# Query and key of two attention pairs by seven products in the first stage, and a new plan of slots for the heads

## The chip, the cores and the metric

The kernel runs on one core of a Trainium2 chip. The metric is the time of one execution on the device in microseconds; a kernel's time is the median of its runs. Of five engines four compute: PE (TensorE, matrix products and transposes), DVE (VectorE), ACT (ScalarE) and POOL (GpSimd); SP (SyncE) issues most of the transfers between DRAM and the on-chip memory. Each engine takes its own instructions in order, and waits with them for what others have to finish first.

## What is computed

One layer of a decoder on 512 tokens of width 2048, in float32. The reference, cut to what matters:

```python
h = rms_norm(x, g_mix)
z = h @ w_in                      # 2048 x 7168
aq, ak, av, rq, rk, rv, rg = split(z)
aq = rotate(rms_norm(heads(aq)) * q_norm)   # 8 heads of 128, attention
ak = rotate(rms_norm(heads(ak)) * k_norm)
a_out = moba_attention(aq, ak, av)          # causal softmax attention
rq, rk = rotate(heads(rq)), rotate(heads(rk)) * 128 ** -0.5
r = retention_chunkwise(rq, rk, rv)         # decayed q k^T v, 8 heads
r_out = silu(rg) * (rms_norm(r) * g_ret)
x = x + concat(a_out, r_out) @ w_o
x = x + (silu(rms_norm(x) @ w_gate) * (rms_norm(x) @ w_up)) @ w_down
x = x + (p @ w_ple_proj) * sigmoid(rms_norm(x) @ w_ple_gate + b)
```

## The kernel before

**Products in three parts.** A float32 number is split into a high and a low part (`split`, L51: the high part on ACT, L54, the low one on DVE, L55), and each product is three matmuls, high by high, low by high, high by low (`mm3`, L72, through L63). A matmul of 512 columns is the unit in which the work is counted below. Weights come from DRAM into `raw`, and their parts are `wh` and `wl`.

**Seven products.** A `Group` (L267) multiplies a matrix by 1024 columns of weights with seven products of half matrices in place of eight. Sums of weight quarters are formed by DVE (`raw<-raw`, L81), the factors of the left side are formed once, and each product goes to two PSUM banks named after X, Y or Z, which `evac` adds into the parts of the result. A group is 7 x 4 units of 12 matmuls, 336. The sums for some later weights (w_gu among them) are formed in DRAM, by moves that POOL issues (`summed`, `move`, L144 to L156).

**Stage 1** (`beside`, L603) computes h from x, the query and key of attention pair 0 in the plain way (`Plain`, L500, 8 units of 24 matmuls), and three groups: the values of the attention, those of the retention, and the gate (`kinds`, L598). Pair 0's query and key are stored to DRAM (`zd`), the values and gates too (`vd`, `sgd`, L596).

**The heads' stage.** Heads go in pairs: four pairs of attention (i = 0 to 3), four of retention (i = 4 to 7). For each pair but the first, `projection` (L684) makes query and key of both heads: 8 units of weights, of which `weights` (L671) keeps three ready, by four accumulators; each accumulator's six matmuls in a unit are one *slot*, so that a projection has 32 slots and 192 matmuls, and seven of them 224 slots. `tick` (L654) counts the slots. At each, the pieces that a plan of numbers has put there (`at_slot`, `heads`, L966) are written into the program ahead of the slot's matmuls. In this stage PE's order is the program's order. So the projection of one pair runs between the pieces of the pair before it, and a piece whose input is late stops PE.

For attention the pieces are (`attend`, L811): `turned`, twice, four 128x128 transposes of query or key into `tp` and a split into `qkH` and `qkL`; `scores` for each of four query blocks into `at`, with DVE's mask (L830), maximum (L832) and scale of it (L834), ACT's exponential into `pt` (L837) and DVE's reciprocal and scaling (L838, L839); `weights_turned`, the transposes of `pt` and their split into PH and PL; `result`, the product with v. Before them `qk_attn` (L768) rotates the pair's four token blocks: `z` (L781) and two `m` (L784) with the rope tables, the reduction of squares (L791), the sum of z and m (L81) and the norm's scale of the keys on ACT (L798). The tables (`rope`, L717 and L720) are made once, from `cs`, `sn` and `sides` that SP loads at the start of the stage (L703 to L715). In the retention `qk_ret` (L864) copies the accumulator, swaps the halves of each head by two transfers on ACT's queue (L876, L877), and rotates.

Each finished pair is turned into factors for the product with w_o (`mixed`, L960): sums and splits on DVE and ACT whose results go to DRAM (`spill`, L214) through four buffers `o`. Behind the heads stand p @ w_ple_proj (L1010 to L1027; its result `pp` is copied out of PSUM by ACT, L1023) and the first group of w_o, whose first 16 slots (`take_over`, L1033) still carry the last pieces.

## Time and profile before

| | us |
|---|---|
| runs | 2341.53, 2346.53, 2344.79 |
| median | 2344.79 |
| profiled execution, its own time | 2341.56 |
| span of the profile | 2339.80 |
| stage 1 with its three groups | 0 to 282 |
| heads' stage, attention pairs | 282 to 541 |
| heads' stage, retention pairs and p @ w_ple_proj | 541 to 714 |
| w_o, feed-forward and the last gate | 714 to 2339.8 |

The profile is of one execution. The busy time of an engine counts its instructions without waits; PEld is the loading of a weight into PE, which runs beside a matmul. The chain that ended last is followed backwards from the last instruction, at each step to what released it; its shares say on what the time lies. A row of the windows has the stretch, its length, then busy time and number of instructions for PE, PEld, DVE, ACT and POOL, the clock granted to PE (1.00 is full), the busy share of the DMA engines, and GB/s. A row of the waits has who waited for what: the sum, how often, and the longest. A row of the timeline has start, length, engine, line, operation, and the idle time before it with what ended it.

### The profile page before, as it was taken

How to read it: one execution, taken by the hardware profiler on the slowest of the kernel's cores; microseconds unless marked ns; L12 is line 12 of the kernel's file. 1: busy time of each engine (PE TensorE's matmuls, PEld its weight loads, DVE VectorE, ACT ScalarE, POOL GpSimd, SP SyncE). 2: the span in 40 equal slices, each digit the busy share in tenths (PEclk: the TensorE clock that was granted, in tenths of full speed). 3: DMA queues.
4: the chain of work that ended last, by engine and by line, in shares of the span. 5: the costliest groups of instructions: out<-in, count | busy, mean ns of one | idle time of the engine just before them, and what ended most of it. 6: DMA issues, size and time to landing. Idle time of an engine off the chain costs nothing.

```text
span 2339.8 us, 29408 instructions
## 1 busy us (share of the span) xinstructions
PE 2307.1 (99%) x10493; PEld 1899.2 (81%) x10493; DVE 1896.3 (81%) x2585; ACT 1200.1 (51%) x1792; POOL 105.3 (5%) x135
## 2 busy tenths in 40 slices
PE   9999999999999999999999999999999999999999
PEld 7888877778887888888888888888888878888877
DVE  8888586666667897888988888889879887788798
ACT  8644454444445566545554554455445443447643
POOL 0000011101011000000000000000000000000000
PEclk9999999999999999999999999999999999999999
DMA  6634736778766879477557754765596775869863
GB/s 241 237 129 169 224 117 175 201 204 255 203 195 235 309 270 366 147 225 237 164 153 229 241 147 157 239 220 155 185 395 201 253 300 198 300 228 360 291 206 126
DMA packets 184099, 519.72 MB, mean 222 GB/s; under 512 B 20496, under 2 KB 33424, under 8 KB 179856
## 3 DMA queue, kind: packets, MB, share of 16 engines
q1 hardware_dynamic: 167296, 463.30, 55.6%
q0 software_dynamic: 13952, 50.34, 10.1%
q10 hardware_dynamic: 2704, 4.20, 0.7%
q8 instruction: 82, 1.34, 0.2%
q14 instruction: 65, 0.53, 0.1%
HBM read 411.86 MB, written 147.85 MB: 239 GB/s over the span
## 4 chain that ended last, share of the span: by engine, by line
PE 81%; DVE 10%; DMA 5%; issue 2%; ACT 2%; SPq 0%; POOL 0%; ACTq 0%; DVEq 0%
PE Y L63 30%; PE Z L63 19%; PE X L63 18%; PE acc L63 9%; DVE wl L55 3%; PE at L63 2%; DVE raw L81 2%; PE tp L68 2%; ACT wh L54 1%; DMA raw<-in_w_dn 1%; DMA raw<-in_w_gu 1%; DMA mix<-o 1%; DMA a<-o 1%; DMA mr<-zr 0%; DVE t L78 0%
## 5 line engine op out<-in xcount | busy, mean ns | idle before, releaser
L54 ACT ACTIVATE wh<-raw 128x1024 fp32r<-128x1024 f32 (+1 forms) x728 | 769.9, 1059 | 853.4 <-PE Y L63 304.3
L55 DVE TENSOR_TENSOR wl<-raw,wh 128x1024 fp32r<-128x1024 f32 (+1 forms) x728 | 885.6, 1218 | 300.1 <-ACT wh L54 297.0
L63 PE MATMUL Y<-wh,s 128*128 128x512 f32 (+1 forms) x1656 | 522.8, 389 | 0.4 <-ACT wh L54 0.4
L81 DVE TENSOR_TENSOR raw<-raw 128x1024 f32<-128x1024 f32 x332 | 399.9, 1217 | 15.2 <-DMA raw<-in_w_dn 5.5
L63 PE MATMUL Z<-wh,s 128*128 128x512 f32 (+1 forms) x1164 | 367.4, 389 | 0.2 <-ACT wh L54 0.2
L63 PEld LDWEIGHTS Y<-wh,s 128*128 128x128 f32 x1656 | 310.1, 188 | 65.0 <-ACT wh L54 1.5
L63 PE MATMUL Y<-wl,s 128*128 128x512 f32 (+1 forms) x828 | 323.5, 391 | 1.7 <-DVE wl L55 1.7
L63 PE MATMUL X<-wh,s 128*128 128x512 f32 x1008 | 319.6, 390 | 2.9 <-ACT pp L1023 2.7
L63 PEld LDWEIGHTS Z<-wh,s 128*128 128x128 f32 x1164 | 218.0, 188 | 44.9 <-ACT wh L54 0.6
L63 PE MATMUL Z<-wl,s 128*128 128x512 f32 (+1 forms) x582 | 229.1, 394 | 2.1 <-DVE wl L55 2.1
L63 PEld LDWEIGHTS X<-wh,s 128*128 128x128 f32 x1008 | 189.5, 188 | 43.1 <-ACT pp L1023 3.4
L63 PE MATMUL X<-wl,s 128*128 128x512 f32 x504 | 197.3, 391 | 0.6 <-DVE wl L55 0.5
L63 PEld LDWEIGHTS Y<-wl,s 128*128 128x128 f32 x828 | 155.5, 188 | 35.0 <-DVE wl L55 3.3
L63 PE MATMUL Y<-wh,r 128*128 128x512 f32 x504 | 165.7, 390 | 1.3 <-ACT wh L54 1.1
L63 PE MATMUL acc<-h,wh 128*128 128x512 f32 x512 | 160.3, 394 | 0.8 <-DVE m L784 0.8
L63 PE MATMUL acc<-wh,h 128*128 128x512 f32 x384 | 130.1, 398 | 1.4 <-DVE m L784 1.1
L63 PEld LDWEIGHTS Z<-wl,s 128*128 128x128 f32 x582 | 109.3, 188 | 26.6 <-DVE wl L55 4.7
L63 PE MATMUL Z<-wh,r 128*128 128x512 f32 (+1 forms) x356 | 116.7, 388 | 0.0
L63 PEld LDWEIGHTS X<-wl,s 128*128 128x128 f32 x504 | 94.7, 188 | 21.0 <-DVE wl L55 1.6
L63 PEld LDWEIGHTS Y<-wh,r 128*128 128x128 f32 x504 | 94.4, 188 | 21.3 <-ACT wh L54 2.1
L63 PEld LDWEIGHTS acc<-h,wh 128*128 128x128 f32 x512 | 92.4, 188 | 17.7 <-ACT z L798 1.2
L63 PE MATMUL acc<-h,wl 128*128 128x512 f32 x256 | 100.3, 392 | 0.0
(225 smaller groups left out, 2887.1 us busy)
## 6 DMA issues: line engine op xcount, KB each, us to landing
raw<-in_w_gu SPq DMA_DIRECT2D x172, 512.0 KB, 5.7
raw<-in_w_dn SPq DMA_DIRECT2D x85, 512.0 KB, 6.1
a<-o SPq DMA_DIRECT2D x154, 256.0 KB, 4.9
raw<-in_wqk SPq DMA_DIRECT2D x63, 512.0 KB, 4.6
s<-a SPq DMA_DIRECT2D x21, 1536.0 KB, 7.5
raw<-in_w_vg SPq DMA_DIRECT2D x48, 512.0 KB, 4.9
raw<-in_w_ow SPq DMA_DIRECT2D x32, 512.0 KB, 5.5
xin<-x SPq DMA_DIRECT2D x60, 256.0 KB, 6.0
```

The lines of the kernel that those rows point to most:

```text
L54: return (nc.scalar.activation(H, src, AF.Copy), nc.vector.tensor_tensor(L, src, H.bitcast(F32), op=ALU.subtract))
L55: nc.vector.tensor_tensor(L, src, H.bitcast(F32), op=ALU.subtract))
L63: ins = nc.tensor.matmul(*args, **kw)
L68: ins = nc.tensor.transpose(o, a, ident)
L81: nc.vector.tensor_tensor(o, a, b, op=ALU.add)
```

## The change

The query and key of attention pairs 1 and 2 (of 0 to 3; the second and third) are computed in stage 1 by a fourth group of seven products (`pairs`), between the values of attention and those of retention. Their blocks are stored to DRAM (`zd[1]`, `zd[2]`), and their norms are computed there: eight stores, 32 squares with a sum on ACT. The heads' stage has five projections, of pair 3 and of the four of retention, 160 slots; the products for w_ple_proj are slots 161 to 176, and the first of w_o 177 to 192. Pairs 1 and 2 are loaded at slots 6 and 24 (four transfers each, behind the split of a unit of weights), and their blocks rotated in place from slots 12 and 27, by the same steps as before. Blocks of pair 0 go through the same function at the start of the stage, with its squares taken in stage 1. The plan now counts slots from the start of the stage. The high part of the retention's query and key is split later (`begin`); the swap of halves is done by two copies on ACT from PSUM. Seven products' parts 5, 3 and 2 of six mixed pairs are spilled through the four `rm` buffers. In the first w_o group the PSUM banks are asked for in the order X0, Z0, Z1, X1. PH and PL are two buffers zeroed once. Of 24 moves for w_gu 14 are issued in stage 1. Matmuls, transposes included, are 10493 before and 10445 after.

```diff
-    def spill(where, k, wait=1):
+    def spill(where, k, wait=1, other=None):
         def sink(p):
-            o = ev_tile("o", 4, (P, 2, 256), dt=F32R)
+            o = other((P, 2, 256)) if other and p in "532" else ev_tile("o", 4, (P, 2, 256), dt=F32R)
             store = lambda: nc.sync.dma_start(where[p][:, k].bitcast(F32), o.bitcast(F32))
             return o[:, 0, :], o[:, 1, :], lambda: later(wait, store) if wait else store()
...
             if first:
-                self.bank[k] = [pools.get("chain" + k, pools["chain"]).tile([P, T], F32, name=k + str(b), tag=k + str(b))
-                                for b in range(2)]
+                def bank(k, b):
+                    return pools.get("chain" + k, pools["chain"]).tile([P, T], F32, name=k + str(b), tag=k + str(b))
+                if self.spread and p == "1":
+                    x = bank("X", 0)
+                    self.bank["Z"] = [bank("Z", 0), bank("Z", 1)]
+                    self.bank["X"] = [x, bank("X", 1)]
+                elif not (self.spread and p == "5"):
+                    self.bank[k] = [bank(k, b) for b in range(2)]
...
+    def pairs():
+        def finish(th, nh, b, part, _):
+            tb = 2 * th + b
+            t = part
+            if (th, nh) == (0, 0):
+                t = ev_tile("o", 4, name="zq")
+                nc.scalar.activation(t, part, AF.Copy)
+            later(1, lambda: nc.sync.dma_start(zd[1 + nh][tb], t))
+            sq = ev_tile("o", 4, name="sq")
+            ms = stat.tile([P, 4], F32, name=f"ms{nh}_{tb}", bufs=1)
+            for j in range(4):
+                c = slice(j * HD, (j + 1) * HD)
+                nc.scalar.activation(sq[:, c], t[:, c], AF.Square, accum_out=ms[:, j:j + 1])
+            nc.vector.tensor_scalar(ms, ms, 1.0 / HD, eps1[:, tb:tb + 1], op0=ALU.mult, op1=ALU.add)
+            power(ms, ms, 4)
+            known[1 + nh][tb] = ms
+        return evacuate(finish)
...
-    kinds = [values(0), values(1), gates()]
-    groups = [Group(lambda kh, nh, u, j=j: w_vg[j, kh, nh, u], range(4), s_h, kinds[j]) for j in range(3)]
-    groups[0].next, groups[1].next = groups[1:]
+    kinds = [values(0), pairs(), values(1), gates()]
+    groups = [Group(lambda kh, nh, u, j=j: w_vg[j, kh, nh, u], range(4), s_h, kinds[j]) for j in range(4)]
+    for j in range(3):
+        groups[j].next = groups[j + 1]
     groups[0].pinned = True
...
+        if i >= 56 and i % 4 == 0 and i < 112:
+            move(gu_moves.pop(0), lead[0])
...
-        pieces.setdefault(slot[0] + n, []).append(fn)
+        assert n > slot[0]
+        pieces.setdefault(n, []).append(fn)
...
-    stream = [wqk[i, u] for i in range(1, 2 * NPAIR) for u in range(NC // 2)] + [pT] + [w_pp[n] for n in range(NS)]
+    tags = ["bd"] * 2 + ["c", "l1"] * (6 * NPAIR)
+
+    stream = [wqk[i, u] for i in range(1, NPAIR + 2) for u in range(NC // 2)] + [pT] + [w_pp[n] for n in range(NS)]
...
-            if gu_moves and slot[0] > 40:
+            if gu_moves and slot[0] > 18 and len(stream) % 2:
...
-    z0 = ap.tile([P, NB, 2, 256], F32R, name="z0", tag="v")
-    for b in range(NB):
-        nc.sync.dma_start(z0[:, b].rearrange("p c e -> p (c e)").bitcast(F32), zd[b])
+    def load_pair(i, by=None):
+        z = raw_pair()
+        for b in range(NB):
+            ins = nc.sync.dma_start(z[b // 2][:, b % 2], zd[i][b])
+            if by is not None:
+                paced(ins, by)
+        blocks[i] = [z[b // 2][:, b % 2] for b in range(NB)]
+        return ins
+
+    blocks = {}
...
+    def in_place(i, b, made, norms):
+        of = blocks[i][b]
+        sq = squares(of) if i == 0 else None
+        m = rm_tile("m", (P, 2, 2, 2, HD // 2))
+        z = of.rearrange("p (s h d) -> p s h d", s=2, h=2)
+        whole, *halves = turn(z, m, of, b)
+        for step in halves + [whole]:
+            step()
+        norms.append(norm(b, sq) if i == 0 else known[i][b])
+        made.append(rotated(z, m, norms[b]))
...
-            accs = [z0[:, b].rearrange("p c e -> p (c e)").bitcast(F32) for b in range(NB)]
+            for b in range(NB):
+                in_place(0, b, made, norms)
+        elif i < NPAIR - 1:
+            at_slot((6, 24)[i - 1], lambda: load_pair(i, lead[0]))
+            for b in range(NB):
+                at_slot((12, 27)[i - 1] + b, lambda b=b: in_place(i, b, made, norms))
...
-            nc.scalar.activation(z, acc, AF.Copy)
-            half = HD // 2
-            nc.scalar.dma_start(m[:half], z[half:])
-            nc.scalar.dma_start(m[half:], z[:half])
...
+            z, m = both[f // 2][:, f % 2], rm_tile("mr")
+            nc.scalar.activation(m[:half], acc[half:], AF.Copy)
+            nc.scalar.activation(m[half:], acc[:half], AF.Copy)
+            nc.vector.tensor_tensor(z, acc, cs, op=ALU.mult)
             nc.vector.tensor_tensor(m, m, sn, op=ALU.mult)
             nc.vector.tensor_tensor(z, z, m, op=ALU.add)
-            H, L = qk_pair()
-            split(H, L, z)
-            made.append((H, L))
-
-        for f, acc in enumerate(projection(False)):
-            evac(f, acc)
+            made.append(parted(z) if i == 2 * NPAIR - 1 else z)
...
+    ATTEND = (((1, four(4), four(8), 16), (10, four(14), four(18), 26)),
...
-        at_slot(17 if i < NPAIR else 20 if i == NPAIR else 8, lambda: v.append(v_of(i)))
...
-            plans = ((12, (15, 16, 19, 20), (19, 20, 23, 24), 27), (21, (25, 26, 39, 40), (29, 30, 42, 43), 46))
-            if i == 0:
-                plans = ((19, (22, 23, 26, 27), (26, 27, 30, 31), 33), (28, (34, 35, 39, 40), (39, 40, 43, 44), 47))
-            for j, (turns, steps_s, steps_w, last) in enumerate(plans):
+            for j, (turns, steps_s, steps_w, last) in enumerate(ATTEND[i]):
...
+        at_slot(MIXED[i], lambda: mixed(i, out))
...
-            if n:
+            if n == NS - 1:
+                t = ev_tile("o", 4, name="pp")
+            elif n:
...
+    groups[-1].ends = groups[0].spread = True
```

How the instructions stand now. On PE, where stage 1 ends and the heads' stage begins, before (Y is a bank of the last group, acc the projection's accumulators, h its left side):

```order
L63 MATMUL Y_2317<-wl,h 128x512
L63 MATMUL Y_2317<-wh,h 128x512 x2
L63 MATMUL Y_2317<-wl,h 128x512
L63 MATMUL Y_2317<-wh,h 128x512
L63 MATMUL acc<-wh,h 128x512
L63 MATMUL acc<-wl,h 128x512
L63 MATMUL acc<-wh,h 128x512 x2
L63 MATMUL acc<-wl,h 128x512
```

After (zr are the rotated blocks of pair 0, tp the PSUM tile for transposes):

```order
L63 MATMUL Y_2959<-wl,h 128x512
L63 MATMUL Y_2959<-wh,h 128x512 x2
L63 MATMUL Y_2959<-wl,h 128x512
L63 MATMUL Y_2959<-wh,h 128x512
L68 MATMUL tp<-ident,zr 128x128 x4
L63 MATMUL acc<-wh,h 128x512
L63 MATMUL acc<-wl,h 128x512
L63 MATMUL acc<-wh,h 128x512 x2
L63 MATMUL acc<-wl,h 128x512
L63 MATMUL acc<-wh,h 128x512
L68 MATMUL tp<-ident,zr 128x128 x4
```

The four transposes of pair 0's query have moved from behind 18 slots of projection to ahead of the first; those of the key stand one slot later.

On SP, the loads at the start of the heads' stage, after (sg is the gate's store of the last products, zr<-z_0_190 to z_3_193 the four loads of pair 1):

```order
L623 DMA sg<-e_2616 128x512
L623 DMA sg<-e_2617 128x512
L711 DMA raw<-in_wqk 128x1024
L753 DMA sides<-in_qk_norm 128x256
L757 DMA sides<-in_mask_c 128x128
L761 DMA cs<-in_rope_c 128x512
L762 DMA sn<-in_rope_c 128x512
L801 DMA v<-v_148 128x2x256 x4
L766 DMA zr<-z_0_190 128x512
L766 DMA zr<-z_1_191 128x512
```

The tables' loads stand behind the last two stores of gates, as before. The loads of pair 0, which stood behind them, are earlier now, and those of pair 1 have come in behind the values.

On DVE, in the first head of the stage, from the split of the first weights (PL) to the scaled weights of the third and fourth query block (pt, 128x384 and 128x512), before:

```order
L55 TENSOR_TENSOR PL<-tp,PH 128x128
L830 TENSOR_TENSOR at<-at,sides 128x128
L832 TENSOR_REDUCE mx<-at 128x1
L834 TENSOR_SCALAR mx<-mx,rs 128x1
L55 TENSOR_TENSOR PL<-tp,PH 128x2x128
L830 TENSOR_TENSOR at<-at,sides 128x128
L838 RECIPROCAL sm<-sm 128x1
L832 TENSOR_REDUCE mx<-at 128x1
L839 TENSOR_SCALAR pt<-pt,sm 128x384
L834 TENSOR_SCALAR mx<-mx,rs 128x1
L838 RECIPROCAL sm<-sm 128x1
L839 TENSOR_SCALAR pt<-pt,sm 128x512
```

After, from the mask of the third query block on; its pt comes seven rows behind the last of these (zr and m are blocks of pair 1 in rotation):

```order
L911 TENSOR_TENSOR at<-at,sides 128x128
L81 TENSOR_TENSOR zr<-zr,m 128x512
L832 TENSOR_TENSOR m<-zr,rope 128x4x64 x2
L830 TENSOR_TENSOR zr<-zr,rope 128x512
L81 TENSOR_TENSOR zr<-zr,m 128x512
L913 TENSOR_REDUCE mx<-at 128x1
L911 TENSOR_TENSOR at<-at,sides 128x128
L55 TENSOR_TENSOR wl<-raw,wh 128x1024
L55 TENSOR_TENSOR PL<-tp,PH 128x2x128
L830 TENSOR_TENSOR zr<-zr,rope 128x512
L81 TENSOR_TENSOR zr<-zr,m 128x512
L55 TENSOR_TENSOR qkL<-tp,qkH 128x512
```

Between mask and pt there now stands the rotation of pair 1, beside the splits of weights and of the second head's query and key. And in slots 28 to 32, after, up to the scaled weights of the third query block (zr is pair 2, z<-acc the projection of pair 3):

```order
L830 TENSOR_TENSOR zr<-zr,rope 128x512
L832 TENSOR_TENSOR m<-acc,rope 128x4x64 x2
L830 TENSOR_TENSOR z<-acc,rope 128x512
L832 TENSOR_TENSOR m<-acc,rope 128x4x64 x2
L915 TENSOR_SCALAR mx<-mx,ms_3_1957 128x1
L830 TENSOR_TENSOR z<-acc,rope 128x512
L830 TENSOR_TENSOR zr<-zr,rope 128x512
L919 RECIPROCAL sm<-sm 128x1
L81 TENSOR_TENSOR zr<-zr,m 128x512
L919 RECIPROCAL sm<-sm 128x1
L81 TENSOR_TENSOR zr<-zr,m 128x512
L920 TENSOR_SCALAR pt<-pt,sm 128x384
```

Two rotations, one from DRAM and one from accumulators, are interleaved ahead of that pt.

185 lines of the change are left out of this document (109 added, 76 removed), and 3 rows, old and new, of the table RETAIN.

## The prediction

> **What bounds the kernel now.** I read the page first: the span, the busy times, and the chain that ended last.
>
> ```profile
> span 2339.8 us, 29408 instructions
> PE 2307.1 (99%) x10493; PEld 1899.2 (81%) x10493; DVE 1896.3 (81%) x2585; ACT 1200.1 (51%) x1792; POOL 105.3 (5%) x135
> PE 81%; DVE 10%; DMA 5%; issue 2%; ACT 2%; SPq 0%; POOL 0%; ACTq 0%; DVEq 0%
> ```
>
> PE is busy 2307.1 of 2339.8 us, so the time is the number of matmuls times their pitch plus 32.7 us in which PE stands. A change pays only by fewer matmuls or fewer stalls. So the next views are the windows by stage and the waits of PE in the two parts of the heads' stage.
>
> ```profile
> 145.00:222.00 77.00, 76.46 (x336) 62.98 (x336) 62.73 (x63) 37.29 (x41) 0.00 (x0) 1.00 0.51 164
> ...
> 282.00:541.00 259.00, 248.29 (x1196) 202.42 (x1196) 179.32 (x416) 120.77 (x238) 40.68 (x41) 1.00 0.63 182
> 541.00:714.00 173.00, 169.09 (x835) 141.86 (x833) 116.05 (x217) 85.21 (x187) 18.21 (x25) 0.99 0.74 227
> ```
> ```profile
> PE tp L68 <- DVE pt L839: 5.1, 7, 1.5
> PE acc L63 <- DVE m L784: 1.9, 3, 0.8
> PE at L63 <- DVE PL L55: 1.5, 1, 1.5
> PE tp L68 <- ACT z L798: 0.8, 2, 0.4
> ```
> ```profile
> PE X L63 <- ACT pp L1023: 2.7, 2, 1.8
> PE acc L63 <- DVE wl L55: 2.3, 1, 2.3
> ```
>
> The first windows row is one group of seven products in stage 1: 336 matmuls, PE idle 0.54 of 77.00 us. In the attention part (second row) PE stands 10.7 us, mostly for the softmax steps of DVE; the first fence of waits is of that part, the second of 541 to 730. The waits named are short: 1.5 us at most there.
>
> **The matmuls.** Two projections of 192 matmuls leave the heads' stage, 384 together, and one group of 336 comes to stage 1: 48 fewer, all of 512 columns. The chain gives the pitch, and the price of opening a group.
>
> ```profile
> 84.92 10.88 PE Z L63 x48
> ...
> 140.81 3.41 DVE raw L81 x3
> 145.40 5.51 PE Z L63 x23
> ```
>
> 48 matmuls take 10.88 us (0.2267 each): −10.9. One more group opens with a short wait on the sums of weights: I take the 0.54 us of the windows row, +0.6. **Stage 1: −10.3.** The new group's sums (16 more on DVE) and 14 of the 24 moves of w_gu that now run there hide under PE, since DVE was busy 62.73 of 77.00 us and the DMA engines 0.51; if the cover fails, 0 to +2, kept for the range.
>
> **The start of the heads' stage** is where I see the largest cost. In the program's order PE now meets the four transposes of pair 0's q directly behind the last product of stage 1; before, 18 slots of projection (a slot is six matmuls) stood between. PE takes its instructions in order, so what the transposes wait for, everything waits for. They need all four rotated blocks, these need the rope tables, and the tables need cs, which SP issues behind the last two stores of gates; those need the last product itself. So this chain cannot start earlier than stage 1's end. Its length stands in the trace of before, where it was covered:
>
> ```profile
> 281.81 0.39 PE L63 MATMUL Y<-wh,h 128*128 128x512 f32 x1
> ```
> ```profile
> 283.93 0.94 SPq L596 DMA_DIRECT2D sg<-e  x2
> ...
> 286.46 0.38 SPq L711 DMA_DIRECT2D cs<-in_rope_c  x1
> ```
> ```profile
> 286.46 5.71 DMA cs<-in_rope_c
> ```
> ```profile
> 292.26 1.29 DVE L717 TENSOR_TENSOR rope<-cs,sides 128x512 f32<-128x512 f32 x2 [1.25 <-DMA cs<-in_rope_c]
> 293.47 1.22 DVE L55 TENSOR_TENSOR wl<-raw,wh 128x1024 fp32r<-128x1024 f32 x1
> 294.61 1.42 DVE L720 TENSOR_TENSOR rope<-sn,sides 128x256 f32<-128x256 f32 x4
> 295.95 0.68 DVE L781 TENSOR_TENSOR z<-z,rope 128x512 f32<-128x512 f32 x1
> 296.55 0.68 DVE L791 TENSOR_REDUCE ms<-sq 128x4 f32<-128x512 f32 x1
> ...
> 300.55 1.76 DVE L784 TENSOR_TENSOR m<-z,rope 128x256 f32<-128x256 f32 x5
> 302.23 0.67 DVE L791 TENSOR_REDUCE ms<-sq 128x4 f32<-128x512 f32 x1
> ...
> 304.82 1.28 DVE L81 TENSOR_TENSOR z<-z,m 128x512 f32<-128x512 f32 x2
> ```
>
> From starts to starts: cs issued 286.46, landed 292.17, first table 292.26. Two table products 293.47 − 292.26 = 1.21; four 295.95 − 294.61 = 1.34; then of the changed kernel's order eight m (1.68 / 5 = 0.336 each, 2.69), four z (0.60 each, 2.40) and four sums (0.60 each, 2.40, by z's pitch). Together 10.04: the blocks are ready at 302.3. The reductions and weight splits that lay between before are done earlier or later now, so I leave them out. PE's last product ends its turn at 281.81 + 0.23 = 282.04: an idle stretch of 20.3 us. What it replaces is the 0.8 us for z and 0.4 for e (a wait listed in the same view): **+19.1**, from 16 (an emptier DMA lands cs in less than its 5.71) to 22.
>
> After so long a rest I expect the clock at half. The trace shows what stalls do to it:
>
> ```profile
> 714.31 0.50 PE L63 MATMUL X<-wh,s 128*128 128x512 f32 x1 [0.96 <-ACT pp L1023]
> ...
> 717.76 0.50 PE L63 MATMUL X<-wh,s 128*128 128x512 f32 x1 [1.77 <-ACT pp L1023]
> ```
> ```profile
> 719.20:722.50 3.30, 3.30 (x10) 2.70 (x10) 2.37 (x7) 1.37 (x2) 1.76 (x2) 0.50 1.05 424
> ...
> 500.00:503.30 3.30, 3.30 (x18) 2.74 (x17) 2.96 (x9) 1.46 (x4) 0.52 (x1) 1.00 0.35 74
> ```
>
> Two waits of 0.96 and 1.77 us at the first group behind the heads were followed by 3.3 us at a granted clock of 0.50; half the work of such a stretch is lost, **+1.7** here, up to 3.4 if it holds for two. The Trainium skill, page "TensorE: Matmul & The Clock Gate", section "Part 1: The HAM clock gate", says that the clock halves after at least one idle window of about 3.4 us and recovers after as much busy time. By that rule the idle start costs the same 1.7, while waits of 0.96 and 1.77 would not have halved it: this trace disagrees there, and by the page alone the 1.7 gained at the first w_ow group (below) would not come, which makes the sum 1.7 worse. I go by the trace.
>
> **The first heads' softmax.** Pair 1's blocks come from DRAM at slot 6, are rotated in slots 12 to 15 of the plan, and in DVE's order this rotation stands among the first head's mask, maximum and scaling steps. DVE also takes them in order. Before, between the mask of the third query block and its scaled weights lay this:
>
> ```profile
> 321.33 0.29 DVE L830 TENSOR_TENSOR at<-at,sides 128x128 f32<-128x128 f32 x1
> 321.65 0.56 DVE L832 TENSOR_REDUCE mx<-at 128x1 f32<-128x384 f32 x1
> ...
> 324.20 0.41 DVE L839 TENSOR_SCALAR pt<-pt,sm 128x384 f32<-128x384 f32 x1
> ```
> ```profile
> 320.65 0.40 PE L63 MATMUL acc<-wh,h 128*128 128x512 f32 x1
> ...
> 327.99 0.49 PE L68 MATMUL tp<-ident,pt 128*128 128x128 f32 x3
> ```
> ```profile
> z<-z SPq DMA_DIRECT2D x8, 256.0 KB, 4.9
> ```
>
> That is 3.3 us of DVE, with 3.4 to spare before PE wanted them at 327.99. Now the same stretch of DVE holds two z and four sums (0.60 each), two m (0.336 each), a weight split (1.14), two qkL (0.60 each, as z), a PL split, two masks (0.29) and two maxima (0.56 and a little more) beside the small steps: 9.4 us by the pitches above, 6.1 more, 2.7 beyond the slack. Ahead of it the rotation stands on its load: this follows a split that is itself behind the first exponential, which I put at 311.7 on before's clock, plus 4.9 is about 317. The first weights' PL behind that comes at 319.9, and PE's slot 10 needs its transpose buffer at some 317: 2.9. The second, ten instructions later, holds slot 11 by 3.8. Together **+9**. Bounds: 0, if loads land early enough that DVE clears the rotation while PE is still in slots 4 to 8 (its share of that stretch is then below one); 12, if each is 1 us later.
>
> The same again in slots 28 to 32: between mask and weights lie pair 2's rotation, pair 3's accumulators (four z, eight m) and the first mixing, 14 us by the same pitches against 7.3 that PE's work covers before (320.65 to 327.99): some 7. With it go the three waits of PE for m, 1.9, at the ends of projections, of which only one projection remains: I take **+6**, from 0 to 10. Other heads keep four slots between scores and weights; I leave their waits as they are.
>
> **What goes elsewhere.** At the first w_ow group the banks are given so that X takes those copied earlier: the 2.7 us for pp goes, and the 1.7 of half clock behind it, **−4.4** (0 if the next wait on POOL's store or a weight takes its place). The retention's half swaps by two copies on ACT instead of a copy and two transfers.
>
> ```profile
> mr<-zr ACTq DMA_DIRECT2D x24, 128.0 KB, 5.1
> ...
> 684.78 0.69 DVE L879 TENSOR_TENSOR zr<-zr,ropeT 128x512 f32<-128x512 f32 x1 [2.19 <-DMA mr<-zr]
> ```
>
> A landing of 5.1 us leaves the chain; ACT, busy 85.21 of 173.00 us there, has room for 32 half copies. DVE's 2.19 is what made the split late for which PE waited 2.3: **−2.5** (0 to −4, if its half clock goes as well). Parts of the mixing kept in another buffer take some waits for stores away: **−1.5** (0 to −4).
>
> Sum: −10.3 + 19.1 + 1.7 + 9 + 6 − 4.4 − 2.5 − 1.5 = +17.1. On the profiled execution (2341.56) that is 2358.7; this stands 3.2 below the runs' median of 2344.79, on which it is 2361.9. I take **2360 us**. About 0.2% (4.7 us) is what a measurement of this kernel can tell from no change; runs of before spread by 5.0.
>
> **The rivals.** *The collisions don't occur (0.17).* DVE has 80 of 259 us free in the attention part and its order is only a queue; if loads land early, the 9 and 6 vanish, and m's 1.9 goes: about +2, 2346. For it: the waits of before are all short. Against: the rows of the order.
>
> *Faster (0.15).* The rotations leave the ends of the projections, where accumulators held PE, and run between, so that the attention's waits (5.1 + 1.9 + 1.5 = 8.5) go as a whole, without collisions: 2344.8 − 10.3 + 20.8 − 4.4 − 2.5 − 1.5 − 8.5 = 2338. It decides if pair 1's rotation is through DVE before slot 8's masks, and pair 2's before slot 28.
>
> *DVE becomes the bound (0.15).* Splits, rotations and softmax put more on DVE in slots 33 to 48 than PE needs for them (118% by my count of its instructions at these durations). With some 22 us of PE there, 18% is +4, and the queues behind lose as much again: with the start 2370.
>
> That fewer matmuls are run is certain from the counts (10493 to 10445); no rival is left there.
>
> **How the numbers follow.** My forecast has 0.53 and its own range is 2350 to 2366. The range of 8 in 10 reaches to most of the faster and slower rivals: 2339 to 2371. Faster 0.15 (the second rival), same 0.17 (the first), slower 0.68 (0.53 + 0.15).
>
> **What would show it.** At the end of stage 1, one idle stretch of PE of 16 to 22 us in front of a transpose, with DVE's sum named as releaser, then a row at clock 0.50. Waits of PE for PL and pt at slots 10 to 12, two to four us each, and in slots 28 to 32. No wait for pp at the first w_ow group. Stage 1 longer by one group (77.0 us), the heads' stage shorter by 87 of matmuls, less its stalls. I am wrong if that first stretch is below 10 us, or if the waits of the attention part stay below 1.5 us each.

## The result, and the profile after

| | before | after |
|---|---|---|
| median of 4 runs, us | 2343.16 | 2365.44 |
| lowest and highest | 2340.91, 2346.53 | 2362.40, 2365.76 |
| ratio, 95% interval | | 1.0088 [1.0076, 1.0099] |
| profiled execution, its own time | 2341.56 | 2362.40 |
| its span | 2339.8 | 2360.6 |
| start of the last product of stage 1 | 281.81 | 359.59 |
| start of the first product of w_o (X) | 714.31 | 732.66 |

The change made the kernel 22.3 us slower; the forecast was 2360 in a range of 2339 to 2371, with 0.68 on slower. Repeated (the last experiment) it was 1.0087 [1.0074, 1.0099], 18.9 us.

The starts in the table cut the program into three parts. Stage 1 is 77.78 us longer, the heads' stage 59.43 shorter (432.50 to 373.07), the rest 2.45 longer (1625.49 to 1627.94): +20.8, the difference of the two spans. The 384 matmuls that left the heads' stage are worth 384 x 0.2267 = 87.05, so without new stalls it would have come to 345.45; it is 27.6 above that. That is the loss to explain. The rest of the program, which the change hardly touches, was between 1624.3 and 1631.0 us in all the traces below, so small effects are read from the heads' stage and not from the sum.

The page after, its first lines:

```profile
span 2360.6 us, 29420 instructions
PE 2300.4 (97%) x10445; PEld 1896.0 (80%) x10445; DVE 1928.0 (82%) x2601; ACT 1230.6 (52%) x1882; POOL 116.2 (5%) x135
```

PE is 6.7 us less busy and the span 20.8 longer: PE stands 60.2 us where it stood 32.7. The windows after, of the new group (`pairs`, 128.6 to 205.5), of a stretch of two later groups and of the heads' stage:

```profile
128.60:205.50 76.90, 76.47 (x338) 63.05 (x336) 60.05 (x63) 41.36 (x84) 7.95 (x9) 1.00 0.49 158
...
222.00:299.00 77.00, 76.57 (x338) 62.89 (x337) 62.31 (x63) 37.70 (x41) 12.68 (x9) 1.00 0.69 219
...
359.80:732.60 372.80, 334.78 (x1645) 279.28 (x1645) 265.04 (x579) 194.14 (x413) 33.52 (x44) 0.95 0.61 186
```

The first two rows are as dense as the group's row of before, though squares run on ACT beside the one and moves for w_gu beside the other. The third row holds the loss: 38.0 us in which PE is not busy, and a granted clock of 0.95 in place of 1.00. The waits of PE after, from 359 to 745 (sum, times, longest):

```profile
PE tp L68 <- DVE zr L81: 17.9, 1, 17.9
PE tp L68 <- DVE pt L920: 11.6, 4, 8.3
PE tp L68 <- DVE r L1022: 4.7, 2, 3.8
PE tp L68 <- DVE PL L55: 3.3, 1, 3.3
```

Before, 18 waits of 1.5 us at most, but for one of 2.3, made 13.8 us in this stage. Now waits at four places make most of 38, and each stands where PE's order meets a transpose. The first is at the start; the timeline after, PE and SP and DVE merged:

```profile
361.71 0.94 SPq L623 DMA_DIRECT2D sg<-e  x2
...
364.21 0.38 SPq L761 DMA_DIRECT2D cs<-in_rope_c  x1
...
369.51 1.29 DVE L774 TENSOR_TENSOR rope<-cs,sides 128x512 f32<-128x512 f32 x2 [1.43 <-DMA cs<-in_rope_c]
...
372.06 2.76 DVE L832 TENSOR_TENSOR m<-zr,rope 128x256 f32<-128x256 f32 x8
...
377.16 2.49 DVE L81 TENSOR_TENSOR zr<-zr,m 128x512 f32<-128x512 f32 x4
377.89 2.28 PE L68 MATMUL tp<-ident,zr 128*128 128x128 f32 x4 [17.92 <-DVE zr L81]
379.83 0.77 PE L63 MATMUL acc<-wh,h 128*128 128x512 f32 x1
```

This is the chain of the prediction, step for step: stores of gates, cs issued behind them, tables, eight m, four z, four sums. From the last product (359.59) to the first of the projection it is 20.24 us, where it was 0.77. The four transposes start with the first sum and then take the blocks as the sums end, which is why the idle time shown is 17.9 and the loss more.

The second place is the first head's softmax. DVE after, from the rotation's start on its load to the scaled weights:

```profile
393.13 1.44 DVE L832 TENSOR_TENSOR m<-zr,rope 128x256 f32<-128x256 f32 x4 [0.80 <-DMA zr<-z]
...
396.84 0.29 DVE L911 TENSOR_TENSOR at<-at,sides 128x128 f32<-128x128 f32 x1
397.05 0.68 DVE L81 TENSOR_TENSOR zr<-zr,m 128x512 f32<-128x512 f32 x1
...
401.32 0.41 DVE L55 TENSOR_TENSOR PL<-tp,PH 128x256 fp32r<-128x256 f32 x1
...
405.68 0.42 DVE L920 TENSOR_SCALAR pt<-pt,sm 128x384 f32<-128x384 f32 x1
```
```profile
401.88 0.63 PE L68 MATMUL tp<-ident,zr 128*128 128x128 f32 x4 [3.25 <-DVE PL L55]
...
406.24 0.52 PE L68 MATMUL tp<-ident,pt 128*128 128x128 f32 x3 [2.34 <-DVE pt L920]
```

From the mask (396.84) to the end of the scaled weights DVE takes 9.3 us, with hardly a gap. Before it was 3.3. PE, in the second fence, stands first for PL and then for pt. The third place is slots 28 to 32, DVE and then PE:

```profile
449.49 0.68 DVE L830 TENSOR_TENSOR z<-acc,rope 128x512 f32<-128x512 f32 x1
450.09 0.68 DVE L830 TENSOR_TENSOR zr<-zr,rope 128x512 f32<-128x512 f32 x1
...
455.26 0.41 DVE L920 TENSOR_SCALAR pt<-pt,sm 128x384 f32<-128x384 f32 x1
```
```profile
455.81 0.87 PE L68 MATMUL tp<-ident,pt 128*128 128x128 f32 x3 [8.35 <-DVE pt L920]
```

The accumulators of pair 3 (z<-acc) and pair 2 (zr) alternate ahead of the pt for which PE waits 8.35 us. The fourth was not foreseen. Near the end of the heads' stage PE waits for r, the result of a retention head. POOL, DVE and PE there:

```profile
704.56 1.09 POOL L1116 DMA_DIRECT2D pp<-pp  x2 [0.44 <-ACT pp L1115]
705.67 1.06 POOL L84 TENSOR_TENSOR rs<-ms,neghalf 128x4 f32<-128x4 f32 x1
```
```profile
703.88 0.20 DVE L1018 TENSOR_SCALAR ms<-ms 128x4 f32<-128x4 f32 x1
...
708.34 0.87 DVE L1022 SCALAR_TENSOR_TENSOR r<-r,rs,sg 128x128 f32<-128x128 f32 x3
```
```profile
708.73 1.26 PE L68 MATMUL tp<-ident,r 128*128 128x128 f32 x4 [3.75 <-DVE r L1022]
```

The sum ms is ready at 704.08 (703.88 + 0.20). Its inverse root (L84) is POOL's, and stands behind stores of pp in POOL's queue until 705.67. That is 1.6 us; POOL's root takes 1.06, and DVE, which has the split of a weight and of a key to do first, comes to r another 1.6 later. The granted clock (third column from the end) behind the wait at 401.88, behind the one at 406.24, and behind the one for r:

```profile
401.90:407.10 5.20, 2.86 (x16) 2.19 (x17) 4.72 (x12) 3.77 (x10) 0.00 (x0) 1.00 0.35 102
407.50:410.50 3.00, 3.00 (x11) 2.41 (x10) 0.89 (x2) 1.55 (x2) 0.00 (x0) 0.50 0.00 0
...
708.00:713.90 5.90, 5.17 (x14) 4.06 (x15) 4.29 (x13) 2.97 (x8) 0.19 (x1) 0.50 1.03 418
```

The wait of 3.25 us at 401.88 left the clock at 1.00. Behind the start and the wait of 8.35 it is 0.50 too (377.9 to 382.5, 455.8 to 460.8). Counted from the rows of PE's matmuls against the pitch at full clock (0.2267 for 512 columns, 0.135 for a transpose), the four stretches lost, in the order of time, 1.6, 1.5, 2.5 and 2.7 us, 8.3 together.

### The profile page after: what moved, and what is told of

It is laid out like the page before. It is cut to its first block, busy times and chain, and to the rows that moved or that the text cites. A ratio compares the mean times of both kernels' runs of the same rounds, so it can differ in the third digit from the quotient of the medians.

```text
span 2360.6 us, 29420 instructions
## 1 busy us (share of the span) xinstructions
PE 2300.4 (97%) x10445; PEld 1896.0 (80%) x10445; DVE 1928.0 (82%) x2601; ACT 1230.6 (52%) x1882; POOL 116.2 (5%) x135
## 4 chain that ended last, share of the span: by engine, by line
PE 53%; DVE 4%; DMA 3%; issue 1%; ACT 0%; SPq 0%; ACTq 0%; DVEq 0%
PE Y L63 23%; PE Z L63 15%; PE X L63 14%; DVE wl L55 2%; DMA raw<-in_w_dn 2%; DVE raw L81 2%; PE tp L68 1%; ACT wh L54 0%; DMA s<-a 0%; DMA raw<-in_w_gu 0%; DMA pp<-pp 0%; DMA xin<-x 0%; DVE e L81 0%; DVE o L55 0%; DVE t L78 0%
## 5 line engine op out<-in xcount | busy, mean ns | idle before, releaser
L54 ACT ACTIVATE wh<-raw 128x1024 fp32r<-128x1024 f32 (+1 forms) x740 | 782.7, 1059 | 873.7 <-PE Y L63 304.8
L55 DVE TENSOR_TENSOR wl<-raw,wh 128x1024 fp32r<-128x1024 f32 (+1 forms) x740 | 900.2, 1219 | 293.5 <-ACT wh L54 292.0
L63 PE MATMUL Y<-wh,s 128*128 128x512 f32 (+1 forms) x1704 | 537.9, 389 | 0.8 <-ACT wh L54 0.8
L81 DVE TENSOR_TENSOR raw<-raw 128x1024 f32<-128x1024 f32 x348 | 419.4, 1218 | 25.1 <-DMA raw<-in_w_vg 10.9
L63 PE MATMUL Z<-wh,s 128*128 128x512 f32 x1212 | 382.4, 389 | 0.2 <-ACT wh L54 0.2
L63 PEld LDWEIGHTS Y<-wh,s 128*128 128x128 f32 x1704 | 319.3, 188 | 66.6 <-ACT wh L54 1.8
L63 PE MATMUL Y<-wl,s 128*128 128x512 f32 x852 | 333.3, 391 | 0.8 <-DVE wl L55 0.7
L63 PE MATMUL Z<-wl,s 128*128 128x512 f32 (+1 forms) x606 | 238.7, 394 | 2.9 <-DVE wl L55 2.7
L63 PE MATMUL Z<-wh,r 128*128 128x512 f32 x372 | 122.0, 389 | 0.0
L63 PE MATMUL Y<-wl,r 128*128 128x512 f32 x260 | 102.4, 394 | 0.5 <-DVE wl L55 0.5
```

The lines of the kernel that those rows point to most:

```text
L54: return (nc.scalar.activation(H, src, AF.Copy), nc.vector.tensor_tensor(L, src, H.bitcast(F32), op=ALU.subtract))
L55: nc.vector.tensor_tensor(L, src, H.bitcast(F32), op=ALU.subtract))
L63: ins = nc.tensor.matmul(*args, **kw)
L81: nc.vector.tensor_tensor(o, a, b, op=ALU.add)
```

## The experiments

The start of the stage. The theory: PE meets transposes whose chain starts at the end of stage 1, and this alone is some 20 us. The rival: take that away and the same time comes back later, because DVE is what bounds these slots.

**Rotation of pair 0 away.**

```diff
-        whole, *halves = turn(z, m, of, b)
-        for step in halves + [whole]:
-            step()
+        if i > 0:
+            whole, *halves = turn(z, m, of, b)
+            for step in halves + [whole]:
+                step()
...
```

> The changed kernel, but pair 0's four blocks are not rotated: the rotation of that pair is left out, so the transposes at the start of the heads' stage need only blocks that were loaded in stage 1. The theory (the start stall is the chain gate stores, cs, tables, rotation, and nothing pays it back): the 17.9 us wait and the half clock behind it (5.3 us at 0.50, some 2.6 lost) go, 19 to 21 us, time 2345 to 2347, and the waits at slots 10 to 12 and 28 to 32 stay at 3.3 + 2.3 and 8.3 us, give or take 1. The rival (DVE is the bound of the first 48 slots, the stall only comes first): at most half is won, 2354 to 2358, and the later waits grow by the rest.

Measured: 2342.73 against 2344.01, 0.9997 [0.9987, 1.0006], which is 22.7 us below the changed kernel's median; the heads' stage 351.85, 21.2 shorter. PE goes from the last product (359.51) to the transposes without a pause; the second fence is the largest of its later waits:

```profile
359.74 0.60 PE L68 MATMUL tp<-ident,zr 128*128 128x128 f32 x4
```
```profile
PE tp L68 <- DVE pt L922: 13.9, 6, 8.8
```

The price of the start, half clock included, is 21.2 (predicted 19.1 + 1.7 = 20.8), and little of it comes back: the later waits for pt, PL and qkL are 17.4 (13.9, 1.3 and 2.2) where they were 15.8 with the rotation.

**The first head at slot 13.** Nothing is left out; the other pieces move back with it. Before the change this head stood at slot 19. The core of the edit:

```diff
-            at_slot((6, 24)[i - 1], lambda: load_pair(i, lead[0]))
+            at_slot((16, 37)[i - 1], lambda: load_pair(i, lead[0]))
...
-    ATTEND = (((1, four(4), four(8), 16), (10, four(14), four(18), 26)),
-              ((21, four(24), four(28), 39), (37, four(41), four(45), 53)),
+    ATTEND = (((13, four(16), four(20), 28), (22, four(25), four(29), 37)),
+              ((31, four(34), four(38), 46), (40, four(43), four(47), 55)),
```

> The changed kernel with the attention's plan pressed together behind a later start: pair 0's first transposes at slot 13 in place of 1, its heads every 9 slots, pair 1's rotation at slots 24 to 27, pair 2's at 43 to 46, nothing left out; from slot 57 on the plan is the old one. The theory: 12 slots, 16.3 us of projection, lie over the 18 us chain; the start stall falls to 0 to 3 us, its half clock goes, the rotations leave the two collisions; against it the heads are closer by a tenth, 2 to 5 us of new short waits. Time 2338 to 2346. The rival (DVE is the bound there): 44 slots must hold what 56 held, DVE falls behind, and 10 us or more come back as waits for pt and PL; 2352 to 2362.

Measured: 2351.83, 1.0032 [1.0017, 1.0047]; the stage 358.33, 14.7 shorter. PE's largest waits:

```profile
381.17 0.33 PE L68 MATMUL tp<-ident,zr 128*128 128x128 f32 x1 [3.18 <-DVE zr L81]
...
433.84 1.09 PE L68 MATMUL tp<-ident,pt 128*128 128x128 f32 x4 [9.02 <-DVE pt L920]
```

Of the start 3.2 stays. But 9.0 us stand now at a pt that DVE has behind the rotations and norms of pair 3's accumulators, since the same heads are left fewer slots. So the rival is half right: products can cover the start, but of the 21.2 that it costs only 14.7 are won in this plan.

The two collisions. The theory: rotations between mask and pt hold PE. The rival: DVE is short of time as a whole, and the waits move but don't vanish.

**Pair 2's rotation seven slots later.**

```diff
-                at_slot((12, 27)[i - 1] + b, lambda b=b: in_place(i, b, made, norms))
+                at_slot((12, 34)[i - 1] + b, lambda b=b: in_place(i, b, made, norms))
```

> The changed kernel with pair 2's rotation at slots 34 to 37 in place of 27 to 30, nothing else. The theory (the 8.3 us wait for pt is the rotation of pair 2 standing in DVE's queue ahead of it): with 6 to 7 us of DVE's work out of the way the wait falls to 1 to 3 us and the half clock behind it goes, 7 to 10 us, time 2355 to 2358. The rival (the projection's accumulators and the mixing of pair 0 hold DVE there, and the rotation must be paid anyway): the wait shrinks by 3 us at most, or comes back as large at the head that follows, 2362 to 2366.

Measured: 2358.21, 1.0064 [1.0049, 1.0079], 7.2 below the changed kernel; the stage 371.04, only 2.0 shorter (4.1 against the changed kernel's repetition, the last experiment). The wait of 8.35 is 3.02 now; the waits of this trace:

```profile
PE tp L68 <- DVE pt L920: 6.6, 6, 3.0
PE tp L68 <- DVE PL L55: 4.8, 2, 3.4
```

So 5.3 of the 8.35 went with pair 2's rotation; in DVE's rows the pt of the 3.0 that are left stands behind pair 3's accumulators. About 3 of the 5.3 stand at other waits now: those for pt and PL were 14.9 together and are 12.7 (6.6, 4.8 and a further 1.3 for PL), and the start cost 0.7 more. The two profiles' spans are 4.9 apart, of which 3.6 lie in the rest of the program (1624.3, the lowest of all), which the edit does not touch. What the edit is worth lies between the stage's 2.0 to 4.1 and the medians' 5.4 to 7.2 (first measurement, repetition).

**Pair 1's rotation away.** The same edit as for pair 0, with i == 1.

> The changed kernel, but pair 1's four blocks are not rotated (the rotation of that pair is left out; its loads and the scale of its keys stay). The theory (the waits at slots 11 and 12 are that rotation in DVE's queue): the 3.3 and 2.3 us and the 3.4 us of half clock behind them go, 6 to 7.5 us, time 2358 to 2360. The rival (they come from the transpose buffers, the weight splits and the first head's own chain): under 2 us, 2363 to 2366.

Measured: 2357.81, 1.0064 [1.0049, 1.0079]; the stage 371.16, 1.9 shorter. PL's 3.25 and pt's 2.34 are one wait of 2.3 now, but the one in slots 28 to 32 grew to 9.6:

```profile
PE tp L68 <- DVE pt L922: 10.5, 3, 9.6
...
PE tp L68 <- DVE mx L917: 2.3, 1, 2.3
```

In this trace the rival has it: PE comes to slot 28 earlier, DVE's queue there does not. But the trace is of the slowest of the four executions (2363.30); against the repetition the stage is 4.0 shorter, and by medians the run is 5.8 to 7.6 faster than the changed kernel. How much of pair 1's price comes back at pair 2 is thus not settled.

**Pairs 1 and 2 both unrotated.** The condition is `1 <= i <= 2`.

> The changed kernel with the rotation of both pair 1 and pair 2 left out (the start stall stays). It bounds what the two rotations cost in all. If the theory holds, the waits at slots 11 and 12 and most of the 8.3 us go together, and with them the half clocks: 9 to 14 us below the changed kernel. If the accumulators and the first head's own chain are the cause, the waits of the runs with one rotation moved or left out stay (2.3 at slot 11 and 3.0 at slots 32 and 33), and 5 to 8 us are won.

Measured: 2354.54 against 2344.74, 1.0047 [1.0033, 1.0061], 9.1 below the changed kernel on the same chip; the stage 365.20, 7.9 shorter than in the first trace of the changed kernel and 9.9 than in its repetition. The waits left:

```profile
PE tp L68 <- DVE pt L922: 3.4, 4, 2.3
PE tp L68 <- DVE mx L917: 2.7, 1, 2.7
PE at L63 <- ACT pt L920: 2.2, 1, 2.2
```

Both rotations with their half clock cost 8 to 10 us. The 8.3 us still waited for here are not theirs: they stand at steps of the softmax in the new slots, and which part of them pair 3's accumulators make was not tested.

The edits elsewhere.

**PSUM banks asked for in the order of before.**

The edit also puts the last copies of pp back into their old buffers, so the two are undone together.

```diff
-            if n == NS - 1:
-                t = ev_tile("o", 4, name="pp")
-            elif n:
+            if n:
...
-    groups[-1].ends = groups[0].spread = True
+    groups[-1].ends = True
```

> The changed kernel with the first w_o group's PSUM banks asked for in the old order, and the last pp copies in the old buffers. The prediction's term: the 2.7 us wait for pp comes back, with 1.7 of half clock, so 2368 to 2371, seen as waits of X for pp at the first w_o group. The rival (with the new plan ACT has copied pp in time, or another wait stands there): no such wait, 2364 to 2367.

Measured: 2366.33 against 2342.99, 1.0100 [1.0083, 1.0117]; by medians no difference that its interval shows. The stage is 378.86, 5.8 or 3.7 longer (first trace, repetition), and the wait is back:

```profile
739.82 0.80 PE L63 MATMUL X<-wh,s 128*128 128x512 f32 x1 [5.07 <-ACT pp L1113]
```

This wait counts as the stage's, because it stands ahead of the first product of w_o. The first 500 matmuls from there on take 2.0 us less than in the changed kernel (110.2 and 112.2), so that 1.7 to 3.8 remain.

**The swap of halves by transfers again.**

```diff
-            nc.scalar.activation(m[:half], acc[half:], AF.Copy)
-            nc.scalar.activation(m[half:], acc[:half], AF.Copy)
-            nc.vector.tensor_tensor(z, acc, cs, op=ALU.mult)
+            nc.scalar.activation(z, acc, AF.Copy)
+            nc.scalar.dma_start(m[:half], z[half:])
+            nc.scalar.dma_start(m[half:], z[:half])
+            nc.vector.tensor_tensor(z, z, cs, op=ALU.mult)
```

> The changed kernel with the retention's halves swapped as before, by a copy of the whole accumulator on ACT and two transfers on its queue. The prediction's term: 2 to 4 us of waits come back where a projection of the retention ends (2367 to 2370). The rival (the new plan leaves some 10 us there between the accumulators and the first scores, which hides a 5 us landing): the waits of PE between 560 and 745 us stay as they are, 2364 to 2367.

Measured: 2376.71, 1.0143 [1.0128, 1.0158], 11 to 13 us slower than the changed kernel; the stage 17 longer, 15 against the repetition. The longest of its waits that the changed kernel does not have:

```profile
750.67 0.79 PE L63 MATMUL X<-wh,s 128*128 128x512 f32 x1 [5.87 <-ACT pp L1116]
```

Beside it stand 2.89 for PL at 588.82 and 2.35 for r at 656.57, also new, each with the clock at 0.50 behind it (590.2 to 593.5, 658.5 to 661.8). The copies on ACT are worth four to five times what the prediction gave them, in this plan; which of its places needs them most was not taken apart.

**The result of pair 6's second head four slots later, and its mixing three.**

```diff
-              ((142, 142, 145, 151, 158), (150, 152, 153, 159, 165)),
+              ((142, 142, 145, 151, 158), (150, 152, 153, 159, 169)),
...
-    MIXED = (28, 56, 81, 104, 126, 151, 168, 191)
+    MIXED = (28, 56, 81, 104, 126, 151, 171, 191)
```

> The changed kernel with one retention head's result (third pair, second head) at slot 169 in place of 165, and that pair's mixing at 171 in place of 168. It tests the new 3.75 us wait for r near 709 us. If the result is simply asked for too early, ahead of POOL's power behind the stores of pp, the wait goes and with it the half clock of 707 to 714.6: 5 to 6 us less, 2359 to 2361. If it is a queue that is late as a whole, the wait moves to the next pieces and at most 1 us is won.

Measured: 2361.65, 1.0083 [1.0065, 1.0101]; the stage 368.75, 4.3 shorter. By medians it is 1.9 to 3.8, which the intervals do not separate from no difference. The waits for r are gone; one for pp is new:

```profile
718.76 0.50 PE L63 MATMUL acc<-wh 128*128 128x512 f32 x1 [2.17 <-ACT pp L1115]
```

**The start moved into stage 1.** Three versions, each on the one before. In the first the tables, pair 0's loads and its rotation are written into the last group of stage 1 (at steps 110 to 115 of `beside`), pair 1's load and rotation are at slots 0 and 5 to 8, pair 2's at 39 and 42 to 45. Its core:

```diff
+        if i == 110:
+            load_pair(0)
+            tables()
+        if 112 <= i < 116:
+            in_place(0, i - 112, *pair0)
...
-            for b in range(NB):
-                in_place(0, b, made, norms)
+            return pair0
...
-                at_slot((12, 27)[i - 1] + b, lambda b=b: in_place(i, b, made, norms))
+                at_slot((5, 42)[i - 1] + b, lambda b=b: in_place(i, b, made, norms))
```

> A version meant to beat both, with nothing left out: the tables are made and pair 0 is rotated in stage 1 (tables in two weight buffers that are free by then, gains and cosines in evacuation buffers), so the first transposes need only what stage 1 has finished; pair 1 is loaded at the end of stage 1 and rotated by slot 8, pair 2 loaded at slot 39 and rotated at 42 to 45; its blocks lie in four of the weight buffers, so the stream of weights has four in place of eight in the first pairs. The theory: start stall gone (21), waits at slots 10 to 12 gone (5.6 and 1.7 of clock), the 8.3 us wait down to the accumulators' share of some 3 to 5 us as in the runs before; 2330 to 2337, faster than the kernel before. The rival (DVE, with 18 us more to do at the end of stage 1, makes the splits of weights late): 5 to 10 us of waits of PE for wl or wh before 360 us, 2338 to 2346.

Measured: 2346.50 against 2342.99, 1.0017 [1.0005, 1.0028]. The heads' stage falls to 348.81, but stage 1 is 9.2 longer (its last product at 368.80). Why, in rows of ACT and PE:

```profile
334.68 0.63 ACT L682 ACTIVATE sq<-zr 128x512 f32<-128x512 f32 x1 [9.64 <-DMA zr<-z]
335.21 1.04 ACT L54 ACTIVATE wh<-raw 128x1024 fp32r<-128x1024 f32 x1
```
```profile
336.30 0.51 PE L63 MATMUL Y<-wh,s 128*128 128x512 f32 x1 [2.66 <-ACT wh L54]
```

The square of pair 0 waits 9.6 us for its load, and the high part of a weight stands behind it on ACT. From 337.0 to 343.7 the clock is 0.50. It is the mechanism of the collisions on another engine: a piece that waits for a transfer, ahead of a split that PE needs. At the stage's end PE waits 3.41 more for the last sums e (373.04), which have come behind pair 1's rotation on DVE.

In the second version the squares are taken in `Plain` where pair 0's blocks are made, the rotation is put behind a split of weights, pair 1's load goes to slot 1 and its rotation to slots 6, 7, 16 and 17 behind a head's scaled maximum, pair 2's to slots 24 and 37 to 40; the third and fourth query block of pair 1's first head get more room; and the result of pair 6 is late as in the run above. Parts of the edit:

```diff
-        sq = squares(of) if i == 0 else None
...
+            with tc.issue_after(lead[0].ins), tc.issue_after(lead[1].ins):
+                in_place(0, i - 112, *pair0)
...
-              ((21, four(24), four(28), 39), (37, four(41), four(45), 53)),
+              ((21, four(24), four(28, 36), 40), (38, four(41), four(45), 53)),
```

> The version meant to beat both, with what the early run lost in stage 1 taken out; nothing is left out. Pair 0's squares are taken where its accumulators are copied, so that no square on ACT waits for a load ahead of a split of weights; its rotation is queued behind the splits of its step; pair 1 is loaded at slot 1 and rotated two blocks at slots 6 and 7 and two at 16 and 17, so that stage 1's last sums are not behind it; pair 2 is rotated from slot 37; the weights of the two blocks that met pair 3's accumulators are asked for four slots later, and the late result is asked for four slots later. The theory: the start stall (20), the two collisions (5.6 and 8.3 and their half clock) and the wait for r (4) are all gone, against 2 to 4 us of new short ones; 2326 to 2336, faster than the kernel before by 0.3 to 0.7%. The rival (DVE is the bound in 300 to 460 us, so that what is moved comes back elsewhere): 2338 to 2348.

Measured: 2335.10 against 2344.74, 0.9965 [0.9953, 0.9977]: faster than before's kernel. The heads' stage is 341.01, stage 1 still 4.1 longer than in the changed kernel. Most of that lies early: PE waits 2.45 us for wl at 78.81, which stands behind four sums of weights (4.63 us) in DVE's queue, and the clock is 0.50 from 80.4 to 83.7. The third version below has the same wait (2.53 at 78.66). The largest wait left in the heads' stage, DVE and PE:

```profile
371.96 0.23 DVE L949 TENSOR_SCALAR PL<-ident 128x128 fp32r<-128x128 f32 x1 [5.40 <-DMA sg<-e]
```
```profile
373.44 0.38 PE L63 MATMUL at<-qkL,qkH 128*128 128x256 f32 x1 [4.00 <-DVE qkL L55]
```

The zeroing of PL waits until the gates' stores have left its memory, and the split of query and key stands behind it.

The third version puts this zeroing behind the second query block's scaled maximum.

```diff
-                    for t in kept_p:
-                        nc.vector.tensor_scalar(t[:, 1408:1536], ident, 0.0, None, op0=ALU.mult)
+                    with tc.issue_after(scaled[0].ins):
+                        for t in kept_p:
+                            nc.vector.tensor_scalar(t[:, 1408:1536], ident, 0.0, None, op0=ALU.mult)
```

> The faster version with one thing moved: the zeroing of PH and PL on DVE is queued behind the second query block's scale, where it stood ahead of the split of pair 0's query and key. In the trace of the faster version PL's zeroing waited 5.40 us for the store of the last gates, and PE 4.00 for qkL behind it. The theory (DVE's queue, not the zeroing itself, is what costs): that wait goes or falls below 1 us, with the half clock behind it if there is one, 3 to 5 us less in the heads' stage, 2329 to 2333. The rival (the split would have been late anyway, by ACT's part of it or the softmax behind it): under 1.5 us, 2333 to 2337.

Measured: 2333.35 against 2344.95, 0.9950 [0.9935, 0.9965]; the heads' stage 338.44, the wait of 4.0 gone. The intervals of the second and third version overlap, so that the third is better is shown by its trace only. Its longest waits from the heads' stage on:

```profile
PE tp L68 <- DVE pt L941: 5.0, 4, 3.4
PE at L63 <- DVE pt L1015: 2.7, 2, 1.7
```

With its pieces so placed, the change is a gain of 11.6 us over the kernel before.

**The changed kernel again**, without an edit.

> The changed kernel once more, unchanged, beside the two others on one chip: by how much do its median and its stages differ from the first time? Expected: the median within 2365 plus or minus 2, stage 1 and the heads' stage within 1 us of the first trace, the rest of the program within 3 us.

Measured: 2363.60 against 2344.74, 1.0087 [1.0074, 1.0099]; the heads' stage 375.13 (373.07 in the first trace), the last product of stage 1 at 361.06 (359.59): both differ by more than the 1 us that was expected. Differences of 2 us between single traces of this stage are therefore no effect.

## Why the prediction was right, by its steps

**Stage 1, −10.3.** Right: 77.78 more there against 87.05 less is −9.3 (−7.8 in the repetition). The new group has the density that was read from the old one's row.

**The start, +19.1, and its clock, +1.7.** Right in place, chain and size: 19.5 by the starts of products, 21.2 with the clock when pair 0's rotation is left out. It is the largest term, and decided the sign.

**The first head's softmax, +9.** Right mechanism, 3.4 too dear before the clock. The prediction's three waits were 2.9, 3.8 and 2.7; the first did not come, the others were 3.25 and 2.34. The step that failed is "plus 4.9 is about 317", the landing of pair 1's load: issued at 390.48, it let DVE start at 393.13, 2.65 us later. DVE's 9.3 us from mask to weights are near the 9.4 that were added up from single rows.

**Slots 28 to 32, +6.** Right: 8.35 less the 1.9 for m is 6.4, and 5.3 of the wait went with the rotation. Its own terms, some 7 less 1.9, make 5, so the 6 that was taken is not their sum. That "Other heads keep four slots between scores and weights; I leave their waits as they are" was too careful: of before's waits for pt, 5.1 us, 0.9 are left beside the two new ones.

**The clock.** "half the work of such a stretch is lost, +1.7 here" was priced once, behind the start. The prediction forecast four more waits (2.9, 3.8, 2.7 and some 7), each longer than those of 0.96 and 1.77 that it had shown to halve the clock, and gave none of them that price. Measured, the four stretches lost 8.3: with the next one the most mis-sized term. Not each wait cost it, since the one of 3.25 left the clock at 1.00. And before's kernel paid it once in this stage too, behind its wait of 2.31 for wl at 690.88, 1.6 us by the same count:

```profile
691.90:695.20 3.30, 3.30 (x9) 2.61 (x8) 3.30 (x8) 0.63 (x2) 0.54 (x1) 0.50 1.02 233
```

**The first w_o group, −4.4.** The wait for pp went, and without the order of banks one of 5.07 returns. But the prediction's own bound, "0 if the next wait on POOL's store or a weight takes its place", is nearer to what happened. From the first product of w_o on, the first 500 matmuls take 112.3 us before and 112.2 after: pieces of the last retention pair wait there now (0.3, 0.9 and 1.3 us). And ahead of it 3.75 us for r are new, with 2.7 of half clock behind them. Moving that result four slots gave 4.3 of the stage back in the trace. Of the 3.75 the rows give POOL's order 1.6; an order of POOL with the root first was not tried.

**The swap, −2.5.** Right in sign. The wait of 2.31 for wl is gone with the 1.6 of half clock behind it, 3.9 together: the bound "if its half clock goes as well" was nearer. Undoing it in the new plan costs 11 to 13. These are not the same quantity: the price was worked out on before's plan, where one split was late. In the new plan more hangs on the copies.

**The mixing through other buffers, −1.5.** Not tested by itself; open. A price of it shows in slots 28 to 32: at 445.36 DVE stood 1.00 us ahead of pair 2's m, until a store of the mixing (mix<-o) had left one of the `rm` buffers.

**The sum** was +17.1; medians give +22.3 and +18.9, the two profiles +20.8. It came close partly by luck, because errors have opposite signs: the clock behind the later waits and r were missing (6.7 and 3.75), the first slots 3.4 too dear, and small waits that the prediction kept are gone. The waits in the stage grew by 23.6 (13.8 to 37.4) and the half clock by 6.7 (1.6 to 8.3), 30.3 together, against 27.6 by the starts. That leaves 2.7 us to the other side; there are ten waits fewer, and around each PE may lose a little more than its row says, but this was not measured apart.

**The rivals.** "The collisions don't occur": false, they are in the rows. (Its sum was off as well: 17.1 less 9, 6 and 1.9 is +0.2, not +2.) "Faster": false as the change stands, since it needs pair 1's rotation through DVE ahead of the masks and pair 2's away from slots 28 to 32. Even with both rotations left out and the start kept, the run took 2354.54 and not 2338, because waits of the softmax stayed. The last versions, which move the rotations and cover the start as well, are faster. "DVE becomes the bound": not as a bound of the whole stage, since 21 us come off by taking the start away. In part it holds: when the start is covered by plain delay, 9.0 us stand at pair 3's accumulators, and with pair 1's rotation alone away, pair 2's place waits longer.

## What to carry to other kernels

When work leaves the engine that bounds a kernel, look first at what that work covered: here 18 slots of products had hidden a chain of 20 us from a load to a transpose, and the saving of 10 us was lost to it twice over. On engines that take instructions in order, read the new order between a producer and the piece that its consumer waits for, and never put a piece that waits for a transfer ahead of a split of weights. Price each new stall of two us and more with a half clock that may follow it, and judge an edit by the stage in which it works where the rest of the program varies more than the effect.

## What the runs showed of the hardware

Waits of two to three us can halve the granted clock, but their length alone does not decide it. The granted clock behind the wait of 2.17 us at 718.76 in the run with the late result, and behind the one of 3.18 at 381.17 in the run with the first head at slot 13:

```profile
719.80:723.20 3.40, 3.40 (x11) 2.82 (x10) 2.88 (x4) 1.82 (x4) 1.54 (x3) 0.50 1.04 408
```
```profile
383.00:385.00 2.00, 2.00 (x6) 1.61 (x7) 2.00 (x5) 1.19 (x4) 0.00 (x0) 0.50 0.80 276
```

Against them stands the 3.25 us wait of the changed kernel, which left it at 1.00. A wait of 2.18 for pp came in the last two versions: in the second (695.94) the clock was 1.00 from 696.0 to 699.4, in the third (692.34) it was 0.50 from 692.7 to 696.0. The Trainium skill, page "TensorE: Matmul & The Clock Gate", section "Part 1: The HAM clock gate", asks for an idle window of about 3.4 us. The 8.35, 3.75 and 17.9 us waits of the changed kernel agree with that, and the 3.25; 2.17 and 3.18 do not, nor do 0.96 and 1.77 before. No wait of up to 1.5 us was seen to do it without a second one near it. With one it can: in the run without pair 0's rotation 1.16 us at 2271.59 and 0.43 at 2272.75 were followed by 0.50 from 2273.3 to 2276.6, while in before's trace 1.14 and 0.44 at the same place were not.

The row with the wait is not always the row with the low clock. Behind the wait of 2.17 the clock was still 1.00 from 718.8 to 719.7; in the long waits of the changed kernel it fell while PE stood (0.50 from 362.9 to 377.8, and from 451.6 to 455.8). In the heads' stage of that trace the stretches at 0.50 are 20.5, 3.4, 10.2 and 6.8 us long; the shortest costs half of its length, 1.7 us, where PE is busy throughout (an estimate; by the matmuls' pitch it was 1.5).

A transfer of four blocks of 256 KB was issued at 390.48, when the DMA engines had been still from 386.0 to 390.4 (busy share 0.00). DVE began on its first block 2.65 us later, where the median of eight transfers of that size (z<-z) over before's run was 4.9. A median of landings is thus no price for one transfer. Here it decided the first of the three waits, by an estimate from the rows: PL was ready at 396.32 and PE's transpose began at 396.63 without a wait; 2.25 us later it would have been 1.9 us late.
